# Loading A by half quadrants, weighing its first block in place, and placing VectorE's sums by a load plan in a 4096-cubed Strassen matmul with GELU

## Chip, cores and metric

One core of a Trainium2 chip. The metric is the device time of one execution in microseconds, best when small. Single executions of one kernel here differ by 1 to 15 us, so small differences are read from medians and from ratios of runs on the same chip.

## The reference

```python
def reference(a, b):              # a, b: 4096 x 4096 float32, normal random numbers
    x = np.matmul(a, b)
    return 0.5 * x * (1 + np.tanh(np.sqrt(2 / np.pi) * (x + 0.044715 * x**3)))
```

## The kernel before

The kernel multiplies in float16 with Strassen's seven products instead of eight. A and B are cut into four quadrants ("11" to "22"). The work is 16 groups, one for each pair of a block of A's rows (4 blocks, `mb`) and a block of B's columns (4, `nb`). A group has 7 products of 4 K-quarters each. One K-quarter is one step of 16 matmuls, about 3.45 us. Groups 11, 13, 14 and 15 cut some products once more ("split" products, 14 shorter steps for two products). The block of A changes after groups 3, 7 and 11.

Float16 is only allowed when the data are well scaled. So the kernel also sums the squares of A's rows and B's columns ("weighing"), compares them late in the program, and a general path would take over if they failed.

The five engines have these jobs. PE multiplies. VectorE (DVE) turns A's tiles (32x32 transposes), forms the operand sums such as A11-A22, and adds product results. ScalarE (ACT) copies accumulators out of PSUM, applies GELU and squares A's rows. GpSimd (POOL) starts the loads, SyncE (SP) the stores.

The parts that the change touches, cut:

```python
def load_a(mb, quad, c, h=None):          # one chunk of 1024 of K, one quadrant: 4 DMAs, runs of 256 values
    ...
    s = pool.tile([P, NX, RUN], F16, name="stage", tag="stage", bufs=2)      # two stage buffers
    ...
def turn_a(mb, quad, c, h=None):          # DVE transposes stage -> aT (one tile per quadrant and chunk)
    ...
def weigh_rows(mb, quad, c, xs):          # ACT: square a row, sum it; the square itself goes to "scrap"
    ...
        nc.scalar.activation(
            weighed[mb, quad, c][:, :RUN], s[:, x, :], ACT.Square, accum_out=weighed[mb, ih][:, k, x : x + 1]
        )
def weigh_half(mb, ih):                   # DVE: add the chunks' sums, waits for ACT's rows
    ...

TURNS = ((2, 2), (3, 3), (5, 2), (6, 2), (8, 0), (9, 0), (10, 2), (11, 2))   # (product, K-quarter); 7.. = next group

def stage_block(mb, turns, turned=True):
    free_at = [0, 0]
    for (quad, c), n in zip(chunks, turns):            # quadrants 11, 12, 22, 21, two chunks each
        do(max(n - LOAD_AHEAD, free_at.pop(0)), load, (load_a, (mb, quad, c)))
        free_at.append(n + 4)
        if turned:
            do(n, turn_a, mb, quad, c)
        for x in range(3):
            do(n + 1 + x, weigh_rows, mb, quad, c, list(range(NX))[x * 6 : (x + 1) * 6])
        if c == CH - 1 and quad in ("12", "21"):
            do(n + 4, weigh_half, mb, int(quad[0]) - 1)
...
# the first block is loaded a second time, late, only to be weighed:
stage_block(0, [first_step[CHECK_GROUP] + 8 + 6 * x for x in range(len(chunks))], turned=False)
...
# where an operand sum is put (groups 6 to 15): as early as buffers allow
            if block and q == PAIR[0][1]:
                places[s] = [ring_place(n, SPLIT_AHEAD, (gi, s, c)) for c in range(CH)]
                e = max(ready, last_a, *(e for _, e in places[s]))
                ...
                for qq in range(QPH):
                    task(e, block_sum, gi, s, oa, qq)          # all four at one step
            ...
                e = max(n - ahead, ready, last_a, free[tag][-AHEAD - 1] + 1)
```

"At step n" is a place in program order. An engine that runs ahead reaches it early, one that is behind reaches it late.

## Time and profile before

| | before |
|---|---|
| time, median of the first 3 runs | 1574.9 us (1574.2 to 1575.2) |
| span of the profiled run | 1572.0 us |
| PE busy | 99% |
| waits of PE between warm-ups and last matmul | 12.2 us, and 1.5 us lost at half clock (wide matmuls 427 ns apart instead of 216) |

The prediction below shows PE's waits and the two long gaps. Here are four lines that it does not show: the page's line of the load queue (packets, MB, share of the time of 16 DMA engines), its line of the row squares (busy us, mean ns, idle before), and two lines of VectorE's timeline shortly before the first long gap.

```profile
q0 software_dynamic: 157024, 249.60, 66.5%
```

```profile
L239 ACT ACTIVATE scrap<-stage 128x256 bf16<-128x256 f16 x512 | 212.8, 416 | 50.1 <-DMA stage<-in_a_dram 35.6
```

```profile
1085.93 0.26 DVE L247 TENSOR_REDUCE stat_a<-rows 128x16 f32<-128x64 f32 x1 [2.91 <-ACT scrap L239]
1086.11 1.21 DVE L832 TENSOR_TENSOR bS<-bK 128x2048 f16<-128x2048 f16 x1
```

The last fence matters later. It is the final row sum of the reloaded first block. It stood 2.91 us in VectorE's queue, waiting for ScalarE's squares, and the B sum after it had to wait too. From there to the gap at 1099 us VectorE has no idle time in its timeline.

### The profile page before, as it was taken

The page shows a single profiled execution, that of the slowest core. Times are in us where ns is not written, and L with a number is a line of the kernel's source. Part 1 is how long each engine was busy: PE and PEld are TensorE (multiplying, and loading weights), DVE is VectorE, ACT ScalarE, POOL GpSimd, SP SyncE. Part 2 cuts the span into 40 slices and gives each one's busy share as a digit, 9 for nine tenths or more (in the row PEclk, how much of TensorE's full clock was granted, in tenths as well). Part 3 has the DMA queues.
Part 4 walks back from the last instruction along what each step waited for, and adds up shares of the span by engine and source line. Part 5 has one row for each costly group of instructions (what it writes and reads, how often), then busy time and mean ns, then how long its engine had stood idle before and what let it go on. Part 6 is the DMA issues. An engine that isn't in the chain of part 4 may idle for free. (4 is left out here: it accounts for less than half of the span.)

```text
span 1572.0 us, 21821 instructions
## 1 busy us (share of the span) xinstructions
PE 1553.1 (99%) x7822; PEld 766.1 (49%) x7822; DVE 1112.0 (71%) x1281; ACT 670.1 (43%) x1670; POOL 391.2 (25%) x682
## 2 busy tenths in 40 slices
PE   9999999999999999999999999999899999999998
PEld 4444444444444444444444444444644457677653
DVE  1697988969888886776755557577654668688853
ACT  1036444338874641212566345563356733232211
POOL 7763433331124300011222112121222111212100
PEclk9999999999999999999999999999999999999999
DMA  9999999994799986799999789998999856978852
GB/s 175 197 217 296 265 318 268 287 201 79 202 228 294 296 321 243 306 324 315 330 339 302 229 277 332 354 353 270 365 279 291 229 173 239 322 257 296 297 211 82
DMA packets 219780, 418.88 MB, mean 266 GB/s; under 512 B 18192, under 2 KB 141072, under 8 KB 200464
## 3 DMA queue, kind: packets, MB, share of 16 engines
q0 software_dynamic: 157024, 249.60, 66.5%
q1 hardware_dynamic: 62640, 167.81, 28.5%
q8 instruction: 63, 1.03, 0.3%
q14 instruction: 53, 0.43, 0.1%
HBM read 333.45 MB, written 167.78 MB: 319 GB/s over the span
## 5 line engine op out<-in xcount | busy, mean ns | idle before, releaser
L418 PEld LDWEIGHTS <-aS 128*128 128x128 f16 x4448 | 435.5, 98 | 533.8 <-issue 7.1
L418 PE MATMUL accX<-bK,aS 128*128 128x512 f16 x1664 | 362.9, 380 | 4.0 <-ACT x L529 4.0
L418 PEld LDWEIGHTS <-aT 128*128 128x128 f16 x1728 | 169.1, 98 | 205.1 <-issue 1.8
L832 DVE TENSOR_TENSOR aS<-aT 128x2048 f16<-128x2048 f16 x188 | 223.2, 1217 | 58.2 <-PE accX L418 47.1
L239 ACT ACTIVATE scrap<-stage 128x256 bf16<-128x256 f16 x512 | 212.8, 416 | 50.1 <-DMA stage<-in_a_dram 35.6
L556 ACT ACTIVATE y<-y 128x512 f32<-128x512 f32 x192 | 119.0, 630 | 270.0 <-DVE y L565 269.9
L217 POOL DMA_DIRECT2D bR<-in_b_dram x320 | 173.2, 543 | 208.5 <-DMA bR<-in_b_dram 117.7
L418 PE MATMUL accY<-bK,aS 128*128 128x512 f16 x1024 | 222.3, 379 | 0.0
L818 POOL DMA_DIRECT2D bK<-k_M x116 | 62.5, 541 | 449.3 <-PE accX L418 121.8
L217 POOL DMA_DIRECT2D stage<-in_a_dram x176 | 111.6, 640 | 240.2 <-ACT scrap L239 188.7
L378 DVE TENSOR_TENSOR aS<-aT 128x2048 f16<-128x2048 f16 (+1 forms) x112 | 133.8, 1199 | 32.3 <-PE accX L418 23.4
L418 PE MATMUL accX<-bS,aS 128*128 128x512 f16 x704 | 153.4, 379 | 1.9 <-DVE bS L378 1.2
L378 DVE TENSOR_TENSOR bS<-bR 128x2048 f16<-128x2048 f16 x110 | 133.6, 1217 | 18.0 <-PE accX L418 9.6
L261 ACT ACTIVATE square<-bR 128x1024 bf16<-128x1024 f16 x120 | 123.0, 1049 | 50.5 <-DVE energy L565 50.3
L529 ACT COPY x<-accX 128x512 f32<-128x512 f32 x120 | 69.5, 586 | 153.4 <-PE accX L418 147.3
L529 ACT COPY m<-accX 128x512 f32<-128x512 f32 x68 | 39.2, 582 | 187.1 <-PE accX L418 175.3
L192 DVE STREAM_TRANSPOSE aT<-stage 128x2048 uint32<-128x2048 uint32 (+1 forms) x37 | 74.5, 2017 | 62.6 <-DMA stage<-in_a_dram 56.5
L832 DVE TENSOR_TENSOR bS<-bK 128x2048 f16<-128x2048 f16 x80 | 96.9, 1216 | 28.6 <-DMA k_split<-bS 28.6
L418 PE MATMUL accY<-bK,aT 128*128 128x512 f16 x512 | 111.8, 379 | 0.0
L418 PE MATMUL accX<-bK,aT 128*128 128x512 f16 x512 | 111.8, 379 | 0.0
L500 PEld LDWEIGHTS <-aS 128*128 128x128 f16 x960 | 93.9, 98 | 17.2 <-issue 2.5
L239 ACT ACTIVATION_READ_ACCUMULATOR scrap<-stage 128x1 f32 x512 | 95.6, 187 | 0.0
(70 smaller groups left out, 1302.9 us busy)
## 6 DMA issues: line engine op xcount, KB each, us to landing
bK<-k_M POOLq DMA_DIRECT2D x116, 1024.0 KB, 11.5
out_dram<-y SPq DMA_DIRECT2D x256, 256.0 KB, 6.6
bR<-in_b_dram POOLq DMA_DIRECT2D x320, 128.0 KB, 7.7
k_M<-bS SPq DMA_DIRECT2D x80, 512.0 KB, 6.7
k_split<-bS SPq DMA_DIRECT2D x80, 512.0 KB, 7.7
stage<-in_a_dram POOLq DMA_DIRECT2D x144, 256.0 KB, 12.3
bK<-k_split POOLq DMA_DIRECT2D x18, 1024.0 KB, 6.6
k_M<-bR SPq DMA_DIRECT2D x16, 1024.0 KB, 12.2
```

Source lines behind the costliest of these rows:

```text
L192: nc.vector.transpose(dst[:, :, x, :], src[:, :, x, :])
L217: nc.gpsimd.dma_start(out=dst, in_=src)
L239: nc.scalar.activation(weighed[mb, quad, c][:, :RUN], s[:, x, :], ACT.Square, accum_out=weighed[mb, ih][:, k, x : x + 1])
L261: nc.scalar.activation(t[:, :], src, ACT.Square)
L378: nc.vector.tensor_tensor(out=x, in0=y, in1=z, op=ALU.add if o[2] > 0 else ALU.subtract)
L418: nc.tensor.matmul(acc[:, :], sa[:, j // 2, i * P : (i + 1) * P, j % 2], sb[:, j, :], start=start and j == 0, stop=stop and j == 3, skip_g ...
L500: nc.tensor.matmul(banks[chain, i][:, :] if wide else out, sa[:, j // 2, r * P : (r + 1) * P, j % 2], sb[:, : NC] if wide else sb[:, j * N ...
L529: nc.scalar.copy(out=t[:, :], in_=src[:, :])
L556: nc.scalar.activation(y[:, :], src[:, :], ACT.Gelu_apprx_tanh)
L818: nc.gpsimd.dma_start(out=t, in_=kept_unit(*key[1:])[:, :])
L832: nc.vector.tensor_tensor(out=t, in0=y, in1=z, op=ALU.add if op > 0 else ALU.subtract)
```

## The change

The intent has three parts. Blocks 1 to 3 of A are read in runs of 512 values (half of a quadrant's rows, all of its K) instead of 256 (all rows, half of K). The first block is weighed while it is staged at the start, each square written over its own input, so that its reload falls away. And operand sums go into steps that a plan of VectorE's load shows as free.

```diff
+BLOCK_AHEAD = 8
-CHECK_GROUP = 9
-TURNS = ((2, 2), (3, 3), (5, 2), (6, 2), (8, 0), (9, 0), (10, 2), (11, 2))
+TURNS = ((2, 2), (3, 3), (5, 2), (6, 2), (7, 2), (8, 1), (10, 1), (11, 1))
 ...
-    a_v = a.rearrange("(x mm) (c g r) -> c g mm x r", mm=Q, g=4, r=RUN)
+    a_v = a.rearrange("(x mm) (h g s) -> h g mm x s", mm=Q, g=4, s=CH * RUN)
 ...
+    def load_half(mb, quad, h):
+        s = pool.tile([P, NX, RUN], F16, name="stage", tag="stage", bufs=2)
+        s = staged[mb, quad, h] = s.rearrange("p (x c) r -> p x (c r)", c=CH)
+        return [(s[g * Q : (g + 1) * Q, :, :], a_v[kh, g, :, x0 : x0 + n, :]) for g in range(4)]
+    def turn_half(mb, quad, h):
+        for c in range(CH):
+            turn_a(mb, quad, c, h)
 ...
+    def weigh_row(dst, src):
+        nc.scalar.activation(src, src, ACT.Square, accum_out=dst)
 ...
-        (0, "A11_0 B12_0 T11_0 B11_0 A21_0 A12_0 B22_0 B21_0"),
-        (4, "T21_0 A22_0"),
+        (0, "A11_0 B12_0 T11_0 W11_0 B11_0 A21_0 A12_0 B22_0 B21_0"),
+        (4, "T21_0 W21_0 A22_0"),
 ...                                         (A load, T turn, W weigh; one row per step at steps 34 to 65)
-    stage_block(0, [first_step[CHECK_GROUP] + 8 + 6 * x for x in range(len(chunks))], turned=False)
+    at(2, 4, 0, weigh_first_half)
+            free_at.append(n + 3)
+            at_step(n, turn_half, mb, quad, h)
+            for x in range(2):
+                at_step(n + 1 + x, weigh_rows, mb, quad, h, list(range(NX // 2))[x * 4 : (x + 1) * 4])
 ...
+    def sum_step(need, first):
+        fit = {n: (work.get(n, 0) + 1) / (1.5 if steps[n][2] in SPLIT else 3) for n in range(first, need)}
+        e = next((n for n in fit if fit[n] <= 1), min(fit, key=fit.get) if fit else need)
+        add_work(e, 1)
+        return e
 ...
-                for qq in range(QPH):
-                    task(e, block_sum, gi, s, oa, qq)
+                for qq in range(QPH):
+                    last_a = sum_step(n, last_a)
+                    task(last_a, block_sum, gi, s, oa, qq)
```

More of the change, by code (lines that the diff above doesn't have):

```diff
@@ L158, in half_path @@
     }
-    checks = {which: iter(range(stats[which].shape[1] // NX)) for which in stats}
-    a_v = a.rearrange("(x mm) (c g r) -> c g mm x r", mm=Q, g=4, r=RUN)
-    b_v = b.rearrange("(c g jj q e) n -> c g e q jj n", g=4, q=Q, e=2, jj=NJ // 2)
+    checks = iter(range(2 * NNB))
+    a_v = a.rearrange("(x mm) (h g s) -> h g mm x s", mm=Q, g=4, s=CH * RUN)
+    b_v = b.rearrange("(h g c jj q e) n -> h c g e q jj n", g=4, c=CH, q=Q, e=2, jj=NJ // 2)
     a_tiles, b_tiles = {}, {}
@@ L179, in load_a @@
         return [
-            (s[g * Q : (g + 1) * Q, x : x + n, :], a_v[kh * CH + c, g, :, x0 : x0 + n, :])
+            (s[g * Q : (g + 1) * Q, x : x + n, :], a_v[kh, g, :, x0 : x0 + n, c * RUN : (c + 1) * RUN])
             for g in range(4)
@@ L187, in turn_a @@
             a_tiles[mb, quad, c] = t
-        s, t = staged[mb, quad, c], a_tiles[mb, quad, c]
         x = slice(0, NX) if h is None else slice(h * NX // 2, (h + 1) * NX // 2)
-        src = s.bitcast(U32).rearrange("p mb (jj q) -> p jj mb q", q=Q)
-        dst = t.bitcast(U32).rearrange("p jj (mb q) -> p jj mb q", q=Q)
-        nc.vector.transpose(dst[:, :, x, :], src[:, :, x, :])
-        if h != 0 and mb == 0:
-            del staged[mb, quad, c]
+        if mb:
+            src = staged[mb, quad, h].rearrange("p x (c r) -> p c x r", c=CH)[:, c]
+        else:
+            src = staged[mb, quad, c][:, x, :]
+        src = src.bitcast(U32).rearrange("p mb (jj q) -> p jj mb q", q=Q)
+        dst = a_tiles[mb, quad, c].bitcast(U32).rearrange("p jj (mb q) -> p jj mb q", q=Q)
+        nc.vector.transpose(dst[:, :, x, :], src)
+    def load_half(mb, quad, h):
+        ih, kh = int(quad[0]) - 1, int(quad[1]) - 1
+        n = NX // 2
+        x0 = (ih * MH + mb * TM) // Q + h * n
+        s = pool.tile([P, NX, RUN], F16, name="stage", tag="stage", bufs=2)
[4 more added lines that the diff above has]
+            turn_a(mb, quad, c, h)
     def load_b(nb, quad, c, h=None):
@@ L204, in load_b @@
         return [
-            (t[g * Q : (g + 1) * Q, e::2, :], b_v[kh * CH + c, g, e, :, :, n0 : n0 + NC])
+            (t[g * Q : (g + 1) * Q, e::2, :], b_v[kh, c, g, e, :, :, n0 : n0 + NC])
             for e in (range(2) if h is None else (h,)) for g in range(4)
@@ L227, in half_path, with weigh_rows, weigh_first, weigh_first_half @@
     weighed = {}
-    def weigh_rows(mb, quad, c, xs):
+    def weigh_row(dst, src):
+        nc.scalar.activation(src, src, ACT.Square, accum_out=dst)
+    def weigh_rows(mb, quad, h, xs):
         ih, kh = int(quad[0]) - 1, int(quad[1]) - 1
-        s = staged[mb, quad, c]
         if (mb, ih) not in weighed:
-            weighed[mb, ih] = pool.tile([P, 2 * CH, NX], F32, name="rows", tag="rows")
-        if xs[0] == 0:
-            weighed[mb, quad, c] = pool.tile([P, RUN], BF16, name="scrap", tag="scrap")
+            weighed[mb, ih] = pool.tile([P, 2, NX], F32, name="rows", tag="rows")
         for x in xs:
-            k = kh * CH + c
-            nc.scalar.activation(
-                weighed[mb, quad, c][:, :RUN], s[:, x, :], ACT.Square, accum_out=weighed[mb, ih][:, k, x : x + 1]
-            )
-        if xs[-1] == NX - 1:
-            del weighed[mb, quad, c], staged[mb, quad, c]
+            r = h * NX // 2 + x
+            weigh_row(weighed[mb, ih][:, kh, r : r + 1], staged[mb, quad, h][:, x, :])
     def weigh_half(mb, ih):
-        k, t = next(checks["a"]), weighed.pop((mb, ih))
+        t = weighed.pop((mb, ih))
         nc.vector.tensor_reduce(
-            out=stats["a"][:, k * NX : (k + 1) * NX],
+            out=stats["a"][:, (2 * mb + ih) * NX : (2 * mb + ih + 1) * NX],
             in_=t.rearrange("p k x -> p x k"), axis=AX.X, op=ALU.add,
         )
+    def weigh_first(quad, c, xs):
+        ih, kh = int(quad[0]) - 1, int(quad[1]) - 1
+        for x in xs:
+            k = ((kh * CH + c) * 2 + ih) * NX + x
+            weigh_row(stats["a"][:, k : k + 1], staged[0, quad, c][:, x, :])
+    def weigh_first_half():
+        t = pool.tile([P, 2 * NX], F32, name="rows", tag="rows")
+        nc.vector.tensor_reduce(
+            out=t[:, :], in_=stats["a"].rearrange("p (k x) -> p x k", k=2 * CH), axis=AX.X, op=ALU.add
+        )
+        nc.vector.tensor_copy(out=stats["a"][:, : 2 * NX], in_=t[:, :])
     def square(blk, quad, c, h):
@@ L270, in weigh @@
         for half in sorted(energy):
-            k, t = next(checks["b"]), energy[half]
+            k, t = next(checks), energy[half]
             pair = t.rearrange("p (e m) -> p e m", e=2)
@@ L299, in verdict @@
     def verdict(row):
-        t = pool.tile([P, RUN], BF16, name="verdict", tag="scrap").bitcast(F32)[0:1, :]
+        t = pool.tile([1, 15], F32, name="verdict", tag="verdict")
         v, ok = t[:, 0:6], t[:, 6:15]
@@ L656, in at, with at_step @@
         before.setdefault(n, []).append((fn, args))
+    def at_step(n, fn, *args):
+        before.setdefault(n, []).append((fn, args))
     for n, whats in (
-        (0, "A11_0 B12_0 T11_0 B11_0 A21_0 A12_0 B22_0 B21_0"),
-        (4, "T21_0 A22_0"),
-        (6, "T12_0"),
+        (0, "A11_0 B12_0 T11_0 W11_0 B11_0 A21_0 A12_0 B22_0 B21_0"),
+        (4, "T21_0 W21_0 A22_0"),
+        (6, "T12_0 W12_0"),
         (8, "A11_1+B12_1+B22_1"),
-        (9, "T22_0 A12_1+B21_1a B21_1b"),
-        (14, "T11_1 A22_1 B11_1"),
-        (16, "T12_1 A21_1"),
+        (9, "T22_0 W22_0 A12_1+B21_1a B21_1b"),
+        (14, "T11_1 W11_1 A22_1 B11_1"),
+        (16, "T12_1 W12_1:0-4"),
+        (17, "W12_1:4-16 A21_1"),
         (18, "S2 S3 T22_1"),
         (23, "T21_1"),
+        (34, "W22_1:0-1"),
+        (35, "W22_1:1-2"),
+        (36, "W22_1:2-3"),
+        (37, "W22_1:3-4"),
+        (38, "W22_1:4-5"),
+        (39, "W22_1:5-6"),
+        (40, "W22_1:6-7"),
+        (41, "W22_1:7-8"),
+        (42, "W22_1:8-9"),
+        (43, "W22_1:9-10"),
+        (44, "W22_1:10-11"),
+        (45, "W22_1:11-12"),
+        (46, "W22_1:12-13"),
+        (47, "W22_1:13-14"),
+        (48, "W22_1:14-15"),
+        (49, "W22_1:15-16"),
+        (50, "W21_1:0-1"),
+        (51, "W21_1:1-2"),
+        (52, "W21_1:2-3"),
+        (53, "W21_1:3-4"),
+        (54, "W21_1:4-5"),
+        (55, "W21_1:5-6"),
+        (56, "W21_1:6-7"),
+        (57, "W21_1:7-8"),
+        (58, "W21_1:8-9"),
+        (59, "W21_1:9-10"),
+        (60, "W21_1:10-11"),
+        (61, "W21_1:11-12"),
+        (62, "W21_1:12-13"),
+        (63, "W21_1:13-14"),
+        (64, "W21_1:14-15"),
+        (65, "W21_1:15-16"),
     ):
@@ L673, in half_path @@
                 before.setdefault(n, []).append((make_sums, (0, 2, int(what[1]), "bS")))
+                continue
+            if what[0] == "W":
+                xs = range(*(int(x) for x in what[6:].split("-"))) if what[6:] else range(NX)
+                before.setdefault(n, []).append((weigh_first, (what[1:3], int(what[4]), xs)))
                 continue
@@ L712, in half_path @@
                 at(gi, 6, 2 * c + 1, load, (load_b, (nb1, "11", c)))
-    chunks = [(quad, c) for quad in ("11", "12", "22", "21") for c in range(CH)]
-    def stage_block(mb, turns, turned=True):
-        def do(n, fn, *args):
-            before.setdefault(n, []).append((fn, args))
-        free_at = [0, 0]
-        for (quad, c), n in zip(chunks, turns):
-            do(max(n - LOAD_AHEAD, free_at.pop(0)), load, (load_a, (mb, quad, c)))
-            free_at.append(n + 4)
-            if turned:
-                do(n, turn_a, mb, quad, c)
-            for x in range(3):
-                do(n + 1 + x, weigh_rows, mb, quad, c, list(range(NX))[x * 6 : (x + 1) * 6])
-            if c == CH - 1 and quad in ("12", "21"):
-                do(n + 4, weigh_half, mb, int(quad[0]) - 1)
-    for gi in range(len(groups) - 1):
-        if groups[gi + 1][0] != groups[gi][0]:
-            stage_block(groups[gi + 1][0], [step_number(gi, s, q) for s, q in TURNS])
-    stage_block(0, [first_step[CHECK_GROUP] + 8 + 6 * x for x in range(len(chunks))], turned=False)
+    at(2, 4, 0, weigh_first_half)
+    halves = [(quad, h) for quad in ("11", "12", "22", "21") for h in range(2)]
+    for gi in range(len(groups) - 1):
+        mb = groups[gi + 1][0]
+        if groups[gi][0] == mb:
+            continue
+        free_at = [0, 0]
+        for (quad, h), turn in zip(halves, TURNS):
+            n = step_number(gi, *turn)
+            at_step(max(n - LOAD_AHEAD, free_at.pop(0)), load, (load_half, (mb, quad, h)))
+            free_at.append(n + 3)
+            at_step(n, turn_half, mb, quad, h)
+            for x in range(2):
+                at_step(n + 1 + x, weigh_rows, mb, quad, h, list(range(NX // 2))[x * 4 : (x + 1) * 4])
+            if h and quad in ("12", "21"):
+                at_step(n + 3, weigh_half, mb, int(quad[0]) - 1)
     for nb, gi in last_raw.items():
@@ L911, in half_path, with add_work, ready @@
     made_at = {}
+    work = {}
+    def add_work(n, amount):
+        work[n] = work.get(n, 0) + amount
+    for n, (gi, s, q) in enumerate(steps):
+        name = product(gi, s)[0] if s >= 0 else ""
+        fresh = gi in SPLITS[M2_M1]
+        tiles = {"M1": 4 if fresh else 8, "M2": 8 if fresh else 4, "M5": 4, "M4": 4, "M6": 4}.get(name, 0)
+        if q in SPLIT:
+            if q in "345":
+                add_work(n + 1, (4 if q == "3" else 2) * 0.33)
+            if q in "76":
+                add_work(n + 1, tiles / 2 * 0.55)
+        elif q == QPH - 1:
+            add_work(n + 1, tiles * 0.55)
+    def sum_step(need, first):
[3 more added lines that the diff above has]
+        return e
+    turned = {}
+    for gi in range(len(groups) - 1):
+        if groups[gi][0] != groups[gi + 1][0]:
+            for (quad, h), turn in zip(halves, TURNS):
+                turned[groups[gi + 1][0], quad] = step_number(gi, *turn)
+                add_work(step_number(gi, *turn), 2.1)
+    def ready(mb, o):
+        return max(turned[mb, quad] for quad in ((o,) if isinstance(o, str) else o[:2]))
     def split_key(gi, s, p):
@@ L929, in half_path @@
         mine = [n for n in range(first_step[gi], first_step.get(gi + 1, len(steps)))]
-        ready = position[gi - 1, NP - 1, 2] if groups[gi][0] != groups[gi - 1][0] else 0
         units, places, users = {}, {}, {}
@@ L940, in half_path @@
                     made_at[nb, s0, PAIR.index((x, p))] = n
+                    add_work(n, 1)
         for n in mine:
@@ L952, in half_path @@
             if block and q == PAIR[0][1]:
-                places[s] = [ring_place(n, SPLIT_AHEAD, (gi, s, c)) for c in range(CH)]
+                places[s] = [ring_place(n, BLOCK_AHEAD, (gi, s, c)) for c in range(CH)]
                 users[s] = []
-                e = max(ready, last_a, *(e for _, e in places[s]))
+                last_a = max(ready(groups[gi][0], oa), last_a, *(e for _, e in places[s]))
                 for c, (x, _) in enumerate(places[s]):
-                    task(e, open_block, gi, s, c, x)
+                    task(last_a, open_block, gi, s, c, x)
                 for qq in range(QPH):
-                    task(e, block_sum, gi, s, oa, qq)
-                last_a = e
+                    last_a = sum_step(n, last_a)
+                    task(last_a, block_sum, gi, s, oa, qq)
             o = SPLIT[q][1] if q in SPLIT else oa
@@ L967, in half_path @@
                 n_a += 1
-                e = max(n - ahead, ready, last_a, free[tag][-AHEAD - 1] + 1)
+                e = max(n - ahead, last_a, free[tag][-AHEAD - 1] + 1)
+                if not block:
+                    e = max(e, ready(groups[gi][0], oa))
                 assert e <= n, steps[n]
+                e = sum_step(n, e)
                 free[tag].append(n)
```

## The prediction

> **What bounds the kernel now.** I read the page's busy shares first, then PE's own waits, then the timeline around the longest of them.
>
> The page's first part:
>
> ```profile
> PE 1553.1 (99%) x7822; PEld 766.1 (49%) x7822; DVE 1112.0 (71%) x1281; ACT 670.1 (43%) x1670; POOL 391.2 (25%) x682
> ```
>
> 7822 matmuls is what the code issues (46 warm-ups and 16 in each of 486 steps), so no record is missing. A busy PE need not be a fast one, so I took the distance from each PE record to the next: 215 to 217 ns for the 512-column matmuls and 108 to 110 ns for the 256-column ones, nearly without exception. The kernel is a stream of matmuls at full rate. Only three things are not that stream: a head of 13.9 us (warm-ups until the first block of A is turned), a tail of some 5 us after the last matmul (last one 1566.8, span 1572.0), and a few gaps. The gaps are PE's waits; columns are the total in us, the number of waits, and the longest.
>
> ```profile
> PE accX L418 <- ACT x L529: 4.7, 2, 4.0
> PE accX L500 <- DVE y L565: 2.4, 1, 2.4
> PE accY L418 <- DVE y L565: 1.8, 2, 1.4
> PE accY L418 <- DVE bS L378: 1.5, 1, 1.5
> PE accX L430 <- DVE table L985: 1.4, 1, 1.4
> PE accX L418 <- DVE bS L378: 1.2, 2, 0.6
> PE accY L449 <- DMA bR<-in_b_dram: 0.6, 1, 0.6
> ```
>
> Without the 1.4 us ahead of the warm-ups these are 12.2 us. After the longest gap seven distances are 427 ns instead of 216, which is 7 x 0.21 = 1.5 us more. So the whole middle holds 13.7 us, 0.87% of the span. **That is the ceiling of any change that leaves the matmuls, the head and the tail alone**, and this one does.
>
> The two long gaps are both in group 11, the first with the halved ("split") products, where a block of A changes too. From the timeline there (start, duration, then the idle time before it and its releaser):
>
> ```profile
> 1089.51 4.62 DVE L832 TENSOR_TENSOR aD<-aT 128x2048 f16<-128x2048 f16 x4
> 1094.05 1.22 DVE L832 TENSOR_TENSOR bS<-bK 128x2048 f16<-128x2048 f16 x1
> ...
> 1097.46 2.48 DVE L565 TENSOR_TENSOR y<-accY,x 128x512 f32<-128x512 f32 x4
> ...
> 1099.39 3.87 PE L500 MATMUL accX<-bK,aS 128*128 128x512 f16 x32 [2.36 <-DVE y L565]
> ...
> 1133.06 0.42 ACT L239 ACTIVATE scrap<-stage 128x256 bf16<-128x256 f16 x1 [11.37 <-DMA stage<-in_a_dram]
> 1133.12 2.31 DVE L192 STREAM_TRANSPOSE aT<-stage 128x2048 uint32<-128x2048 uint32 x1 [9.82 <-DMA stage<-in_a_dram]
> ...
> 1136.18 2.02 ACT L529 COPY x<-accX 128x512 f32<-128x512 f32 x4
> 1136.79 5.56 PE L418 MATMUL accX<-bK,aS 128*128 128x512 f16 x18 [4.01 <-ACT x L529]
> ```
>
> First gap: four sums of a block (aD) come in one burst, and the adds that empty accY stand behind them. Second gap: ACT's queue stood 11.37 us on a load of A, then squared six rows, and only then copied accX, for which PE waited. Neither gap is for want of an engine's throughput; both are questions of order.
>
> **What the Trainium skill says.** "TensorE: Matmul & The Clock Gate", part 1: the clock falls to half after about 3.4 us of idle and needs about as long to return; warm, 512 columns take 215.7 ns. The trace agrees: 216 ns, and 427 ns only behind the 4.01 us gap, not behind the 2.36 us one. "Perfetto Trace Analysis", Tensor Engine Instruction: ACT and DVE are strict FIFO. The trace agrees: the accX copies at 1136.18 were ready since about 1132.8 but stood behind the row squares. "DMA: Bandwidth & Descriptors", Specifications: transfers of 512 B reach line rate. The trace differs: in its DMA records a 512-byte packet of the load queue takes 63 ns on average and a 1024-byte one 100 ns, so doubling the run saves 21% of the time for the same bytes.
>
> **The change part by part.**
>
> *Half quadrants in runs of 512 (blocks 1 to 3 of A).* A load of four DMAs still brings 1 MB as f16, in 1024 packets instead of 2048. By the packets above that is 2048 x 63 / 16 = 8.1 us before (the four landings around 1125 to 1133 span 7.9 us) and 1024 x 100 / 16 = 6.4 us after: 1.7 us earlier for the last of four. One turn of 2048 columns (2.30 us) becomes two of 1024 (2.37 us for a pair at the start of the run): no change for DVE. Rows become 8 of 512 instead of 16 of 256. ACT squares 256 columns in 416 ns and 1024 in 1049, so 512 take about 0.63 us; with the accumulator read the row pitch is 0.54 us now and I estimate 0.75. That is 6.0 us for a half instead of 8.6. But the square now overwrites the stage tile, so it must wait for both turns; today it needs only the load.
>
> *Reload removed.* 32 DMAs of 256 KB go, around 890 to 1075 us: 16384 packets x 63 / 16 = 65 us of all DMA engines, and 128 rows x 0.54 = 69 us of ACT. The timeline has no PE gap there, so this is worth nothing on the path.
>
> *First block weighed in place.* The same 69 us of ACT come at the start. From 0 to 80 us ACT is busy 6.2 us, so there is room, but the two stage buffers are now held until a chunk is squared. I laid the 8.6 us batches over the timeline: chunk one 12 to 21 us (its buffer is wanted at 22.6), the second until 34.6 (wanted 39.1), the third until 45.7 (wanted 45.7), the fourth until 54 (wanted 59.6), the fifth until 74.2 (wanted 73.2), the sixth until 82.8 (wanted 81.9). Two loads slip by 1 us. The accX copies at 81.37 move to about 82.8, and the turn at 81.27 slips 1 us in front of the product at 83.76, with about 1 us of slack: I book +0.7 us. The single rows later, one per step of 3.45 us, are 0.54 us each and hidden.
>
> *Sums by a load plan, block places 8 steps ahead.* The same operand sums of 1.22 us each. The four block sums move from one burst into steps with less DVE work. The first long gap should go (-2.4 us), and the B sum at 1094.05, which frees the buffers fetched next, can come up to 4.6 us earlier.
>
> *Turns.* The "22" half ends at step (1,1) of the next group instead of (2,0), three steps ahead of its product. Two gaps at 447 and 455 us (0.62 and 0.68 us) lie right behind the turn of that chunk at 443; they should go, and part of the 0.39 us at 398: -1.0 us.
>
> *The second long gap.* The load lands 1.7 us earlier by its packets; the squares wait 2.4 us for the turns; four rows (3.0 us) stand before the copies instead of six (3.2 us): +0.5 us by itself. PE arrives 2.4 us earlier, the fetches ahead of the load up to 4.6 us earlier. So the gap comes out at 4.0 + 0.5 + 2.4 - (0 to 4.6) = 2.3 to 6.9 us. Compared with gap plus slow clock now, and with the first gap already booked, I take the favourable half: -1.5 us.
>
> Sum: -2.4 - 1.0 - 1.5 + 0.7, and +0.3 for a chance that a new ACT wait opens (below): -3.9 us. 1574.9 - 3.9 = 1571.0.
>
> **Rivals.**
> (1) *The gap is only moved.* Loads land one after another, about 2.8 us apart, from 1100 to 1165: in this stretch the DMA queue is the limit. If A lands at the same time, the 2.4 us gained at 1099 are waited for at 1133. For it: the DMA line near 9 and ACT's 11.37 us. Against it: fewer packets and an earlier B sum. Then about 1574.
> (2) *All waits of group 11 go*, and the clock stays full: -2.4 - 4.0 - 1.5 - 1.0 + 0.7, about 1567. For it: the change is aimed at these. Against it: the first load is still asked for only 6 steps before its turn, four of them short ones.
> (3) *A new ACT wait at each change of block.* The second half of "22" is loaded 4 steps ahead of its turn, not 6 (its buffer is free no sooner), and its rows are squared just before the m copies that release accX. Landings at the second change of block took 13 to 22 us; 4 steps are 13.8 us. Two changes with 2 us each: about 1575 to 1577.
> (4) *The start loses.* If held stage buffers delay loads in a chain, 3 to 6 us: about 1576. The queues have 1 to 5 us of slack there by the above.
>
> **Range and chances.** The floor is 1574.9 - 13.7 = 1561. With (2) and (3) or (4) as the ends and the 1 us by which runs differ, 1564 to 1578 should hold 8 in 10. Faster by 2% would be under 1543.4, below the floor: 0.01. Slower by 2% needs 31 us of new waits, over twice all of today's: 0.03. Within 2%: 0.96.
>
> **What would show it.** Right: PE's wait for DVE y in group 11 gone, aD sums scattered, no stage load in 890 to 1075, row squares near 0.63 us, stage packets half as many, a PE wait on the x copies left near 1130 but shorter. Wrong: new PE waits before 120 us (the start), waits of ACT on stage in front of m or x copies at each change of block (rival 3), or the x wait as long as before (rival 1). A second half-clock stretch would add 1.5 us at a blow.

## The result, and the profile after

Ratios here and below are the mean time of one kernel's fast runs over that of the other's fast runs of the same rounds, so they are not quite the ratio of the medians quoted.

| | before | after |
|---|---|---|
| median, call of the result | 1574.56 us (1573.1 to 1575.2, 4 runs) | 1577.61 us (1574.7 to 1581.5, 4 runs) |
| ratio, call of the result | | 1.0022 (0.9999 to 1.0046) |
| ratio, later call (13 runs of after, see after_again) | | 1.0002 (0.9992 to 1.0011) |
| span of the profile | 1572.0 us | 1576.5 us |
| PE distances over the normal one: at gaps / at half clock | 13.7 / 1.5 us | 16.4 / 3.9 us |

No gain; the two ratios stand for a loss of 3.5 and of 0.3 us, and neither is clear of noise. The prediction had said 1571.0. Distances, from the start of one matmul to the start of the next, give more than the profile's waits (13.7 us at gaps before, not 12.2), since a wait is counted only from the modelled end of the matmul before it. In what follows a gap is named by the time, in us from the start of the span, at which the matmul behind it starts; the recorded expectations name some gaps by their begin, 2 to 3 us earlier. The page's first line and PE's waits of the changed kernel:

```profile
PE 1555.3 (99%) x7822; PEld 765.7 (49%) x7822; DVE 1114.9 (71%) x1305; ACT 586.6 (37%) x1286; POOL 364.6 (23%) x650
```

```profile
PE accX L443 <- DVE bS L403: 5.3, 3, 2.7
PE accX L443 <- DVE aS L892: 2.2, 1, 2.2
PE accY L443 <- DVE y L590: 1.8, 1, 1.8
PE accX L443 <- DVE aS L403: 1.6, 1, 1.6
...
PE accX L443 <- ACT m L554: 1.2, 2, 0.8
PE accY L443 <- DVE bS L403: 0.8, 1, 0.8
```

The two long waits of before (4.0 us for ACT x, 2.4 us for DVE y) are gone. Others stand in their place. **Group 11** is now as planned; its timeline shows two block sums (aD) ahead of the adds that empty accY (the other two follow at 1103.81), and a turn of A that waits for nothing:

```profile
1099.02 2.35 DVE L892 TENSOR_TENSOR aD<-aT 128x2048 f16<-128x2048 f16 x2
1101.29 2.60 DVE L590 TENSOR_TENSOR y<-accY,x 128x512 f32<-128x512 f32 x4
...
1133.76 2.36 DVE L196 STREAM_TRANSPOSE aT<-stage 128x1024 uint32<-128x1024 uint32 x2
```

**Group 8**, the first after the second change of block, has a gap that was not there. From the timeline of POOL, VectorE and PE:

```profile
814.77 2.33 POOL L232 DMA_DIRECT2D stage<-in_a_dram  x4 [3.84 <-ACT stage L246]
...
832.28 2.37 DVE L196 STREAM_TRANSPOSE aT<-stage 128x1024 uint32<-128x1024 uint32 x2 [8.79 <-DMA stage<-in_a_dram]
...
834.58 3.46 DVE L892 TENSOR_TENSOR aS<-aT 128x2048 f16<-128x2048 f16 x3
...
835.82 3.63 PE L443 MATMUL accX<-bK,aS 128*128 128x512 f16 x16 [2.15 <-DVE aS L892]
```

Read it from the top. POOL waited until ScalarE had squared the rows that held the stage buffer. Only then could it load the second half of quadrant 22, which landed at 832.1. VectorE stood 8.79 us at that half's turn with the next sums behind it. PE waited for the first of those sums. **Group 4** shows the same chain after the first change of block:

```profile
437.98 2.37 DVE L196 STREAM_TRANSPOSE aT<-stage 128x1024 uint32<-128x1024 uint32 x2 [6.13 <-DMA stage<-in_a_dram]
...
446.58 1.22 DVE L403 TENSOR_TENSOR bS<-bR 128x2048 f16<-128x2048 f16 x1
...
447.81 5.52 PE L443 MATMUL accX<-bS,aS 128*128 128x512 f16 x17 [2.06 <-DVE bS L403]
```

**The start** has a gap at 85.5 us. Its load stood on a stage buffer that was being squared:

```profile
73.50 4.57 POOL L232 DMA_DIRECT2D stage<-in_a_dram  x8 [3.29 <-ACT stage L246]
```

```profile
85.54 1.47 PE L443 MATMUL accX<-bS,aS 128*128 128x512 f16 x6 [1.57 <-DVE aS L403]
```

By stretch, in distances over the normal one and with half clock: the start (to 165 us) costs 4.8 us before and 10.8 after; groups 3 to 5 cost 2.2 before and 4.6 after; group 8 nothing before and 3.5 after; groups 11 to 15 8.2 before and 1.1 after. These sum to +4.8 us, against 4.5 us between the two spans. They are of one execution each: that of after was at the kernel's median of this call, but 2.5 us over that of the later one.

The load queue and the row squares went as expected:

```profile
q0 software_dynamic: 115552, 241.21, 60.5%
```

```profile
L246 ACT ACTIVATE stage<-stage 128x512 f16<-128x512 f16 x192 | 118.1, 617 | 89.6 <-DVE aT L196 87.4 <-issue 2.2
```

### The profile page after: what moved, and what is told of

Read it like the earlier page. It is cut to its first block, busy times and chain, and to the rows that moved or that the text cites. A ratio compares the mean times of both kernels' runs of the same rounds, so it can differ in the third digit from the quotient of the medians.

```text
span 1576.5 us, 21403 instructions
## 1 busy us (share of the span) xinstructions
PE 1555.3 (99%) x7822; PEld 765.7 (49%) x7822; DVE 1114.9 (71%) x1305; ACT 586.6 (37%) x1286; POOL 364.6 (23%) x650
## 5 line engine op out<-in xcount | busy, mean ns | idle before, releaser
L246 ACT ACTIVATE stage<-stage 128x512 f16<-128x512 f16 (+1 forms) x320 | 169.4, 531 | 124.8 <-DVE aT L196 120.6
L443 PE MATMUL accX<-bS,aS 128*128 128x512 f16 x704 | 156.8, 385 | 6.8 <-DVE bS L403 4.8
L196 DVE STREAM_TRANSPOSE aT<-stage 128x1024 uint32<-128x1024 uint32 (+1 forms) x61 | 76.0, 1278 | 71.9 <-DMA stage<-in_a_dram 70.3
L232 POOL DMA_DIRECT2D stage<-in_a_dram x144 | 84.6, 593 | 167.0 <-ACT stage L246 135.4
L590 DVE TENSOR_TENSOR y<-accY,x 128x512 f32<-128x512 f32 x68 | 45.2, 688 | 57.4 <-PE accY L443 31.5
## 6 DMA issues: line engine op xcount, KB each, us to landing
k_M<-bR SPq DMA_DIRECT2D x16, 1024.0 KB, 12.2
```

The lines of the kernel that those rows point to most:

```text
L196: nc.vector.transpose(dst[:, :, x, :], src)
L232: nc.gpsimd.dma_start(out=dst, in_=src)
L246: nc.scalar.activation(src, src, ACT.Square, accum_out=dst)
L443: nc.tensor.matmul(acc[:, :], sa[:, j // 2, i * P : (i + 1) * P, j % 2], sb[:, j, :], start=start and j == 0, stop=stop and j == 3, skip_g ...
L590: nc.vector.tensor_tensor(out=o[:, :], in0=x[:, :], in1=y[:, :], op=op)
```

## The experiments

My first theory: the plan brings all of the gain in group 11, the half quadrants add the gaps in groups 4 and 8, the in-place weighing adds the gaps at the start. The rivals were that the plan moves a gap only, that the start is slow for other reasons, and that the late loads are late because the DMA queue is full. The first call had one kernel for each; the second undid or isolated the half quadrants; the third tested what had been learned about the reload. All runs compared were of the fast state, each call on one chip with its own runs of the kernel before. The changed kernel itself ran only in the call of the result and in the second call, so e2 and e4, of the first, are compared with it by ratios across chips. A profile shows one execution and not the median one: those of e1, e8, after_again and the first of e5 are of the slowest run of their call, that of e4 of its fastest. Here profiles say where time is lost, and the times how much.

### e1: the load plan alone

```diff
 (the kernel before)
+BLOCK_AHEAD = 8
+    work, add_work, sum_step as in the change; a chunk's readiness from its own turn
-                for qq in range(QPH): task(e, block_sum, ...)
+                for qq in range(QPH): last_a = sum_step(n, last_a); task(last_a, block_sum, ...)
+                e = sum_step(n, e)            # for every operand sum
```

> The kernel before with only the load plan of VectorE's sums and the block places 8 steps ahead; loads, turns and reload as before. My theory: the plan alone closes the two long gaps of group 11 (2.4 + 4.0 us and 1.5 us of slow clock), and leaves the gaps before 160 us and around 447 to 455 us as they were. So about -7 us, 1567 to 1569 us, and a profile whose PE waits are the 12.2 us of before less 6.4. Rival: the plan only moves the gap to the load of A, and it takes the larger packets or the new turns to close the second gap; then 1571 to 1575 us, with PE waiting for ACT x near 1130.

Measured: 1569.45 us (1567.7 to 1571.4), ratio 0.9965 (0.9952 to 0.9977), so -5.5 us. PE's waits and VectorE's timeline:

```profile
PE accY L419 <- DVE bS L379: 2.5, 1, 2.5
PE accX L501 <- DVE aS L833: 2.4, 3, 2.0
```

```profile
1087.12 0.26 DVE L248 TENSOR_REDUCE stat_a<-rows 128x16 f32<-128x64 f32 x1 [2.97 <-ACT scrap L240]
```

The 4.0 us gap is gone, without larger packets and without new turns. So the rival falls; the gain is 1.5 us less than I had said. The experiment keeps three things together (sums by load, block places 8 steps ahead, a sum ready with its own chunk), and no run parts them. I had not foreseen that a gap of 2.0 us stays near 1100, now for a sum instead of the y adds. Ahead of it stands the same row sum of the reload, again waiting 2.97 us.

How the plan closed the second gap shows in the DMA issues, in us from the start of group 11. Before, five of the B fetches go out together at 4.2 to 7.0, behind a B sum that came at 2.6 after the burst of block sums. With the plan that sum comes at -1.8, and the same five fetches go out at -0.3 to 2.5. The load of A is issued at nearly the same point (20.0 before, 19.2 here) but lands at 33.3 instead of 41.6. Its turn is needed at about 35. That an earlier sum freed buffers earlier, and so emptied the queue in front of the load, is how I read these two traces; no run moved that one sum alone.

### e2: the changed kernel with the first block weighed by a reload again

```diff
-            if what[0] == "W": ... weigh_first ...
-    at(2, 4, 0, weigh_first_half)
+    for k, (quad, h) in enumerate(halves):          # reload in half quadrants
+        n = first_step[9] + 8 + 6 * k
+        at_step(max(n - LOAD_AHEAD, free_at.pop(0)), load, (load_half, (0, quad, h)))
+        ... weigh_rows at n + 1, n + 2; weigh_half at n + 3
```

> The changed kernel with the first block of A weighed by a reload in groups 9 to 11 again (in half quadrants), nothing weighed at the start. My theory: what the change loses before 165 us (about 5.7 us by the profile: 1.6 + 0.4 at 84 to 87 us, 0.3 more at 113, 2.2 more at 157 and the slow clock after it) comes from stage buffers held until their rows are squared. Then PE's gaps before 165 us are those of the kernel before (4.1 us in all) and the time is about 5 us under the changed kernel, 1571 to 1573 us. Rival: the start is slower for another reason (chance in the order of DMAs, other strides of A and B); then it stays at 1576 to 1578 us, with the gap near 157 us.

Measured: 1576.39 us (1572.1 to 1587.6, 22 runs), ratio 1.0020 (1.0007 to 1.0032). A miss. The changed kernel's gaps at 85.5 and 160.6 us did go from its profile, and what is left at gaps before 165 us is 6.0 us, no more than with the plan alone; a stretch of half clock behind the gap at 130 us adds 1.5 us:

```profile
PE accX L443 <- DVE bS L403: 3.1, 2, 2.1
PE accY L443 <- DVE bS L403: 2.6, 1, 2.6
PE accX L443 <- DVE aS L899: 2.0, 1, 2.0
PE accY L443 <- DVE y L590: 1.8, 1, 1.8
```

But the time did not follow. The gaps of groups 4 and 8 are still there, and three stretches of half clock (that one and one behind each of those gaps) add 5.1 us in this profile. So the start was not what kept the changed kernel from its gain.

### e3: in-place weighing alone

```diff
 (the kernel before)
-    stage_block(0, [...], turned=False)
+    the W entries at steps 0 to 65, weigh_first in place, weigh_first_half
```

> The kernel before with only the first block weighed in place while staged, its reload taken out; loads of the later blocks, turns and sums as before. My theory: the same losses at the start as in the changed kernel and no gain, since the reload lay beside other work: +5 us, 1578 to 1581 us, with group 11's two gaps still there. Rival: taking the reload's traffic out helps the stretch around 1070 to 1135 us, the second gap shrinks, and the time stays at 1573 to 1576 us.

Measured: 1574.50 us (1572.3 to 1578.1, 14 runs), ratio 1.0001 (0.9991 to 1.0011). The rival was right in time, though not in the gap it named. The second gap of group 11 is still there (3.7 us, for ACT x). The first one is gone, with sums placed as before:

```profile
PE accX L433 <- ACT x L544: 4.4, 2, 3.7
```

So the reload did cost something on the path: its last row sum in VectorE's queue pushed everything in front of group 11 back by 2.9 us. Taking it out closes a gap of 2.4 us. What takes that gain back is only in part seen: in this profile the start loses 1.1 us more than in that of the kernel before, and the ratio's interval reaches about 1.5 us each way.

### e4: the changed kernel with rows squared one step earlier

```diff
-            free_at.append(n + 3)
+            free_at.append(n + 2)
-                at_step(n + 1 + x, weigh_rows, ...)
+                at_step(n + x, weigh_rows, ...)
```

> The changed kernel with the rows of the later blocks squared one step earlier (at the turn and the step after it), so that a stage buffer is free one step earlier. My theory: the new gaps at 445 us (2.1 us and 1.7 of slow clock) and 833 us (2.2 + 0.8) come from the second half of 22 being loaded too late because its stage buffer is still held by unsquared rows; with the load 3.5 us earlier or more, both shrink to under 1 us: about -4 us, 1572 to 1574 us, the start unchanged. Rival: the load is late because the DMA queue is full; then it lands no sooner and the gaps stay, 1576 to 1578 us.

Measured: 1581.35 us (1578.0 to 1584.2), ratio 1.0045 (1.0031 to 1.0060), slower still. The gap near 835 us is gone, so the held buffer was indeed what delayed that load. But ScalarE now stands at a turn just before it should copy accumulators, and PE waits for those copies:

```profile
PE accX L443 <- ACT x L554: 3.8, 3, 2.9
PE accX L443 <- DVE bS L403: 2.7, 2, 1.5
PE accX L443 <- ACT m L554: 2.5, 3, 1.4
```

The longest is at 363 us, after the turn of (2, 2), and in its wake the clock was at half for 1.7 us. An in-place square must wait for the turn of its tile, where a square into scrap waits only for the load. This profile is of the fastest of the six runs and has no more gaps in all than the changed kernel's, so it shows where new waits came, not the whole of the loss.

### e5: plan and in-place weighing, without half quadrants

```diff
 (e1 and e3 together: the changed kernel with A in chunks, runs of 256 and the turns of before)
```

> The load plan and the in-place weighing of the first block together, without the half quadrants (A in chunks and runs of 256, the turns of before). My theory by now: the plan closes the 4 us gap of group 11, taking the reload out closes the 2.2 us gap at 1097 that was left with the plan alone, and the start loses about 1 us; the half quadrants are what makes the changed kernel lose this again. So about 1567 us (1565 to 1569), ratio near 0.995, gaps in groups 4 and 8 as in the kernel before. Rival: the in-place weighing costs the start 3 to 5 us, as in the profile of the changed kernel; then 1571 to 1575 us with gaps at 84 and 157 us.

Measured: 1568.11 us (1567.1 to 1571.1), ratio 0.9954 (0.9937 to 0.9971). In the third call again: 1568.37 us, ratio 0.9960 (0.9946 to 0.9973).

> Plan and in-place weighing without half quadrants once more, beside the early reload on the same chip. My theory: 0.994 to 0.997, with gaps near 84 and 160 us of 1.5 to 3 us in the profile that the early reload doesn't have; so the early reload is equal or up to 3 us faster. Rival: without the reload there is less traffic and it is faster than the early reload by 1 us or more.

The changed kernel ran in the same call as the first of these and had 1.0002. So the half quadrants cost it 0.48%, about 7.6 us. Under that name go the layout, the new turns and the squares of blocks 1 to 3 written in place; e5 keeps chunks, the old turns and scrap for these blocks. PE's waits in the first of the two profiles:

```profile
PE accX L434 <- DVE bS L394: 2.7, 2, 2.1
PE accY L434 <- DVE y L581: 2.2, 2, 1.8
PE accX L434 <- DVE aS L394: 1.7, 1, 1.7
```

Its longest waits are at the start (86, 116, 131 and 161 us); those at 116 and 131 us the kernel before has too, at 113 and 128 us. In the second profile of the same kernel the gap at 86 us is 0.3 us over the normal distance instead of 1.9, and that at 161 us is missing.

### e6: the changed kernel with quadrant 22 in chunks of K again

```diff
-TURNS = (..., (7, 2), (8, 1), (10, 1), (11, 1))
+TURNS = (..., (8, 0), (9, 0), (10, 1), (11, 1))
+        return load_a(mb, quad, h) if quad == "22" else load_half(mb, quad, h)
+        if quad == "22": return turn_a(mb, quad, h)         # one chunk of K; sums need only their own chunk
```

> The changed kernel with quadrant 22 of the later blocks back in two chunks of K (runs of 256), turned at the steps of before; the other three quadrants stay halves in runs of 512. My theory: a product that follows the turn closely can start on the first chunk of K when the second is still on its way, but needs both halves of the rows' quadrant before its first sum; this alone makes the gaps of 2.2 us near 445 and 833 us and the slow clock behind them. So they go (under 1 us left in each) and the time falls by 4 to 6 us against the changed kernel, 1570 to 1573 us. Rival: the gaps come from where the load stands in the DMA queue or from VectorE being full; then they stay or move, 1576 to 1579 us.

Measured: 1569.60 us (1567.4 to 1575.9, 11 runs), ratio 0.9971 (0.9959 to 0.9984), so about 4.9 us under the changed kernel of the same call. In its profile the gap of group 8 is gone and that near 445 us is down from 2.2 to 0.8 us over the normal distance, with no half clock behind it. PE's waits:

```profile
PE accX L450 <- DVE bS L410: 4.6, 3, 2.8
PE accY L450 <- DVE y L597: 1.8, 1, 1.8
```

The 2.8 us is at 160 us, at the start. One quadrant of four thus makes most of the loss. The run changes its layout and its turns together, since the layout forces the turns; the two were not parted. Product M7 uses A12-A22 right after the block changes. In chunks of K, its first two K-quarters need only the first chunk, and the second is turned at the product's first step. In halves of the rows, every K-quarter needs both halves, so both must be turned before the product begins.

This profile also shows part of what is left. Quadrant 21 is still in halves here, and a gap at 483 us stays (1.35 us over the normal distance). All six profiles with halves of 21 have it, at 483 to 491 us with 0.7 to 2.0 us, and none of the six without. In each, the turn of the second half of 21, one step earlier than the turn of the second chunk was, stands in VectorE's queue ahead of a B sum for which PE waits. With chunks (before, e5) that B sum comes first and the turn after it. The timeline of after_again has it at its largest:

```profile
485.89 2.36 DVE L196 STREAM_TRANSPOSE aT<-stage 128x1024 uint32<-128x1024 uint32 x2
...
489.41 3.61 PE L443 MATMUL accX<-bS,aT 128*128 128x512 f16 x16 [1.86 <-DVE bS L403]
```

### e7: half quadrants alone

```diff
 (e2 with sums placed as in the kernel before)
```

> Half quadrants in runs of 512 with their new turns alone: sums placed as before, first block weighed by a reload (in halves). My theory: nothing of group 11 is gained except what shorter packets give, and the gaps of groups 4 and 8 are added: about 1580 us (1577 to 1584), ratio 1.002 to 1.006. Rival: larger packets close the second gap of group 11 by themselves; then 1573 to 1576 us.

Measured: 1581.75 us (1580.7 to 1583.9), ratio 1.0045 (1.0030 to 1.0061), +7.1 us.

```profile
PE accX L443 <- ACT x L554: 5.5, 1, 5.5
PE accX L443 <- DVE bS L403: 3.9, 2, 2.0
PE accX L443 <- DVE aS L899: 2.5, 1, 2.5
```

The longer runs do not close the second gap of group 11; it grows from 4.0 to 5.5 us. A's load lands 2.8 us earlier here (38.8 instead of 41.6 from the start of the group), but PE arrives 2.5 us earlier too since the first gap is gone, and the squares now wait for the turns. The first gap went with the reload still there and the sums placed as before: the reload's last row sum stands one step earlier in program order than before (n + 3, not n + 4), its squares are done by then, and it does not wait.

```profile
1088.37 0.19 DVE L258 TENSOR_REDUCE stat_a<-rows 128x16 f32<-128x32 f32 x1
```

The three parts measured alone, plan -5.5, in-place without reload 0.0, halves +7.1, sum to about +1.7 us. The whole change measured +3.5 and +0.3 us by its two ratios.

### after_again: the changed kernel once more

> The changed kernel once more, for more runs and a second profile. My theory: the ratio stays 1.001 to 1.004; the gaps near 445 and 833 us and none in group 11 come again; the gaps before 165 us differ by a few us from the first profile, since they depend on which transfer lands first. Rival: the first profile was unlucky, the new one shows no gap over 1 us in groups 4 and 8, and the ratio is under 0.998.

Measured: 1575.60 us (1573.0 to 1579.5, 13 runs), ratio 1.0002 (0.9992 to 1.0011): slightly under the range that I gave, and not the rival. In its profile the gaps near 447 and 835 us come again (at 449 and 837), none over 0.4 us in group 11, and 3.7 us at 162.

### e8: the plan, A in chunks, and the reload begun 28 us earlier

```diff
 (e1)
-    stage_block(0, [first_step[CHECK_GROUP] + 8 + 6 * x for x in range(len(chunks))], turned=False)
+    stage_block(0, [first_step[CHECK_GROUP] + 6 * x for x in range(len(chunks))], turned=False)
```

> The load plan with A in chunks, the reload of the first block kept but begun 8 steps (28 us) earlier, so that its last row sum does not stand in VectorE's queue just ahead of group 11. My theory: the reload costs something only through that one sum, which waited 2.9 us for ScalarE at 1086 us; moved, the 2.0 us gap at 1100 us and the slow clock behind it go, the start keeps its short gaps, and the time is 1565 to 1567 us, ratio 0.993 to 0.995, the best so far. Rival: the reload's traffic, not the sum, is what delays group 11; then the gap stays and the ratio is 0.996 as with the plan alone.

Measured: 1567.07 us (1565.2 to 1567.9), ratio 0.9947 (0.9933 to 0.9960): the best of all kernels run. Moving the reload, with all of its traffic, closes the gap near 1100 us. Alone this would not tell the row sum from the loads and squares that moved with it; that it is the wait of the row sum rests on e7, where the reload began at the same step and its row sum did not wait, and on VectorE's queue in e1, which has no idle time between that wait and the gap. PE's waits here:

```profile
PE accY L419 <- DVE bS L379: 2.4, 1, 2.4
PE accY L419 <- DVE y L566: 2.2, 2, 1.8
...
PE accX L419 <- ACT x L530: 0.7, 1, 0.7
PE accX L501 <- DVE aS L833: 0.7, 3, 0.2
```

Whether e8 beats e5 is not settled. In this call all five runs of e8 lie under all five of e5 (means 1.7 us apart), but the intervals of their ratios overlap, and e5 had 0.9954 in its first call. Both beat the kernel before and the changed one.

## Why the prediction was right or wrong

The forecast gain of 3.9 us did not come. 1577.6 us lies at the upper edge of the stated range, and the later call has no difference at all.

- **What bounds the kernel**: right. PE runs at 216 ns per wide matmul, and every difference in the profiles is a gap or half clock. The ceiling of 13.7 us added PE's waits (12.2) and half clock (1.5); by distances it is 15.2 us. It was never passed; the best kernel gained 8.1 us.
- **Sums by a load plan**: right in mechanism, too small in size. I booked -2.4 and -1.5 us. In the changed kernel all of the 8.2 us of group 11 (over the normal distances, with half clock) went, but for 0.4. The earlier B sum came 4.4 us earlier in e1 and A landed 8.3 us earlier against the group, where I had counted on up to 4.6.
- **The reload "is worth nothing on the path"**: wrong. I looked for PE gaps between 890 and 1075 us and stopped there. Its last row sum stood 2.91 us at 1085.93, and e3, e7 and e8 all show that the first gap of group 11 goes when that wait goes.
- **First block in place, +0.7 us**: too small in the changed kernel's profile, not shown in its times. I took 73.2 us as the time at which the fifth batch's buffer was wanted. That is when the second half of the next load was issued before; the first half was issued at 70.15. The trace shows the eight DMAs of both halves released together at 73.50, after the last of the 16 rows, so the load slipped by 3.3 us instead of 1. Over the start, without half clock, the profiles without it have 4.8 to 6.2 us over the normal distances (five profiles), those with it 5.7 to 10.1 (seven), so the two overlap. In time the difference is within the noise: e3 against the kernel before includes the reload's gain, and e2 against the changed kernel shows no gain.
- **Turns, -1.0 us: the step that failed.** I wrote that the gaps behind the turn of 22 at 447 and 455 us should go since that quadrant was turned three steps ahead. In the sum I did not ask whether its load could be there. In place of -1.0 us, the profile has +2.4 us in groups 3 to 5 and +3.5 us in group 8: the load of the second half of 22 was issued 3.84 us late because its buffer was held, and VectorE stood 8.79 us at its turn. The turns of 22 move from steps (8, 0) and (9, 0) to (7, 2) and (8, 1), while the stage buffer comes free only one step earlier after a turn. Rival 3 had just this (loaded 4 steps ahead, landings of 13 to 22 us) and named "about 1575 to 1577", but I gave it only +0.3 us in the sum. The half quadrants as a whole measured +7.1 us alone (e7) and 7.6 us in the changed kernel (e5), of which 4.9 us go when 22 is in chunks again (e6). The detail differed: PE waits first for VectorE's sums behind the late turn (2.15 us in group 8), then for the m copies (0.77 us).
- **The second long gap**: my "+0.5 us by itself" for in-place squares that wait for the turn was right in sign. In e7 that gap is 1.5 us longer. My 7.9 us for the four landings before is counted from the landing of the fetch ahead of them; the four themselves lie 4.5 us apart (1128.58 to 1133.04). A row of 512 took 0.62 us from one to the next, not 0.75.

Still open: why the start varies by 3 to 4 us between profiles of the same kernel, and what makes up the part of the half quadrants' cost that is not quadrant 22 (7.6 less 4.9 us, with intervals of 2 to 3 us each way). The turn of 21 near 483 us is one piece of it, of 0.7 to 2.0 us.

## What to carry to other kernels

A tile layout fixes what must be complete before the first use. Cutting a load along K lets a product begin on the first piece; cutting it along rows to get longer runs asks for everything at once, and here that cost more than the cheaper packets gave (about a fifth less time for the same bytes). In a kernel whose first engine is 99% busy, look at which instruction stands in front of which in the queues of the others: one 0.26 us row sum at the wrong place cost 2 us and more. And when three changes come together, measure each alone; here one part was worth 5.5 us and another took it back.

## What the Trainium skill lacked or had wrong

- "TensorE: Matmul & The Clock Gate" (part 1, and the table under "Why this matters for your kernels", which asks for no gaps over about 3 us): in these traces 2.2 us without matmuls were enough, and where they fell decided. By the clock records of all twelve traces, a stretch of half clock lasted 3.41 us (one in e7 twice that) and cost about 1.7 us, and all began on a grid of 3.413 us counted from the first release of the clock; that the window runs freely, the page says. I summed the time over the normal distances in each window of that grid. All 13 windows with 2.17 us or more were followed by half clock; of those at full clock with 2.06 us or less, none was. So the 2.2 us gap of e1 at 1100 us, inside one window, cost its half clock, while the gap of 2.5 us at 1099 us in the kernel before, cut by the edge of a window into 2.06 and 0.47 us, cost none. The page has a whole window of idle, about 3.4 us, as the condition.
- "DMA: Bandwidth & Descriptors" (Specifications): 512 B is not line rate for these float32 to float16 loads. By the DMA records of the changed kernel a 512-byte packet took 62 ns, a 1024-byte one 101 ns, and an 8192-byte one of the fetches, which do not convert, 355 ns, so 124, 101 and 44 ns per 1024 bytes. These are bytes as written; the float32 reads of the loads are twice as many, and by bytes read the three are 62, 51 and 44 ns.
- No page of the skill has the cost of a row sum on ScalarE. The square took 416 ns for 256 columns and 617 ns for 512, the read of the accumulator 187 ns more as an instruction of its own. The pitch of rows of 256 was 0.54 us with the square written to a scrap tile and 0.40 us written in place; why was not tested.
